# Rotary embedding on one core: GpSimd's two sine products per tile become one, and VectorE's program is padded to a 128-slot boundary

## The chip, the cores and the metric

The kernel runs on one core of a Trainium2 chip. The core has five engines with instruction streams of their own: TensorE (PE in the profile, its weight loads PEld), VectorE (DVE), ScalarE (ACT), GpSimd (POOL) and SyncE (SP). Sixteen DMA engines move data between the device memory (HBM) and the core's on-chip memory SBUF. PSUM is a second, smaller on-chip memory, which TensorE writes.

The metric is the device time of one execution in microseconds. Three runs of the kernel before gave 163.29, 163.35 and 163.39.

## The reference

The input `x` is float32 with 8 batches, 2048 positions, 8 heads and 64 elements per head. `cos` and `sin` have 32 elements per position. Each head's vector is split into halves and rotated:

```python
x1 = x[..., : x.shape[-1] // 2]
x2 = x[..., x.shape[-1] // 2 :]
out1 = x1 * cos - x2 * sin
out2 = x1 * sin + x2 * cos
return np.concatenate([out1, out2], axis=-1)
```

The input has 33.55 MB and the output as much.

## The kernel before, in words

The 2048 positions lie on the 128 partitions, 16 to a partition (`R` = 16). A batch is one SBUF buffer `xt` of 128 x 8192 elements, and there are five such buffers (`NBUF`). SyncE's queue loads batches 0 to 4 at the start, batch 0 in three pieces with the cosine table behind the first (lines 66 to 69); ScalarE's queue loads the sine table (line 76). Batch `b + 5` is loaded into the buffer of batch `b` once that batch has been stored (line 193). Stores go out on ScalarE's queue, and on SyncE's for the last batch (line 73). The first batch is stored in pieces of 1, 1 and 2 MB, the last in 2, 1 and 1 MB, the others as 4 MB.

A batch is worked off in tiles of 128 x 2048 elements (`UNIT`, four positions per partition). Batch 0 begins and batch 7 ends with two tiles of 128 x 1024 (lines 170 to 175). For each tile `rotate` makes two products and adds them. `t1` is `x` times the cosine, made by VectorE (line 129). `t2` is `x` with its halves exchanged, times the sine, with a minus sign in the first half of each head. In the usual kind of tile, A, GpSimd makes `t2` in two instructions (lines 120 to 127): the second half of each head is `x1` times `sin_sb`, the first half `x2` times `nsin`, which is the negated sine table. VectorE then adds `t1` and `t2` into `xt` (line 136). `t1` of such a tile lies in PSUM.

The first tile of each of batches 1 to 5 is of another kind. In kind B (batches 2, 4 and 5) TensorE makes the sum, as products with the identity `eye` that accumulate in PSUM, and ScalarE copies it back (lines 143 to 145). In kind C (batches 1 and 3) VectorE also makes the sine product (line 148) from a copy of the sine table in PSUM, and TensorE adds or subtracts with `eye` and `neye`. In B and C `t1`, and in C also `t2`, lie in the two SBUF buffers of the pool `t1s`.

GpSimd's `t2` tiles have three buffers (`t2_pool`), so GpSimd can run at most that far ahead of VectorE. The order of work is the order of the program on each engine (`keep`).

Before the loop, GpSimd makes the identity, ScalarE the negated sine table `nsin` (line 90), the PSUM copy `sin_ps` (line 91) and `neye` (line 92), and VectorE the PSUM copy of the cosine table (line 93).

Of the kernel before, what the change touches and what calls it, by code (L numbers as in the profile page):

```python
# [9 lines left out]
@with_exitstack  # L10
def kernel(
    ctx: ExitStack,
    tc: tile.TileContext,
    x: bass.AP,
    cos: bass.AP,
    sin: bass.AP,
    out: bass.AP,
):
    nc = tc.nc
    keep = tc.keep_in_program_order  # L20
    f32 = mybir.dt.float32
    PSUM = bass.MemoryType.PSUM

    B, S, H, D = x.shape
    Dh = D // 2
    P = 128
    HD = H * D
    R = S // P
    ROW = R * HD
    UNIT = 4 * HD  # L30
    NBUF = 5
    C = 512
    last = B - 1

    xv = x.rearrange("b (q r) h d -> b q (r h d)", q=P)
    ov = out.rearrange("b (q r) h d -> b q (r h d)", q=P)
    cos_src = cos.rearrange("(q r) d -> q r d", q=P)
    sin_src = sin.rearrange("(q r) d -> q r d", q=P)

    const_pool = ctx.enter_context(tc.tile_pool(name="const", bufs=1))  # L40
    tab_pool = ctx.enter_context(tc.tile_pool(name="tab", bufs=1, space=PSUM))
    t1_pool = ctx.enter_context(tc.tile_pool(name="t1p", bufs=1, space=PSUM))
    o_pool = ctx.enter_context(tc.tile_pool(name="op", bufs=1, space=PSUM))
    t1s_pool = ctx.enter_context(tc.tile_pool(name="t1s", bufs=2))
    xpool = ctx.enter_context(tc.tile_pool(name="xpool", bufs=NBUF))
    t2_pool = ctx.enter_context(tc.tile_pool(name="t2p", bufs=3))

    cos_sb = const_pool.tile([P, R, Dh], f32, tag="cb")
    sin_sb = const_pool.tile([P, R, Dh], f32, tag="sb")
    nsin = const_pool.tile([P, R, Dh], f32, tag="ns")  # L50
    eye = const_pool.tile([P, P], f32, tag="eye")
    neye = const_pool.tile([P, P], f32, tag="neye")
    cos_ps = tab_pool.tile([P, R, Dh], f32, tag="cp")
    sin_ps = tab_pool.tile([P, R, Dh], f32, tag="sp")

    xts = {}

    def spans(sizes):
        lo = 0
        for n in sizes:  # L60
            yield lo, n
            lo += n

    def load(b):
        xt = xpool.tile([P, ROW], f32, tag="xt", name=f"xt{b}")
        for lo, n in spans([UNIT, UNIT, 2 * UNIT] if b == 0 else [ROW]):
            keep(nc.sync.dma_start(out=xt[:, lo : lo + n], in_=xv[b, :, lo : lo + n]))
            if b == 0 and lo == 0:
                keep(nc.sync.dma_start(out=cos_sb, in_=cos_src))
        xts[b] = xt  # L70

    def store(b, lo, n):
        queue = nc.sync if b == last else nc.scalar
        keep(queue.dma_start(out=ov[b, :, lo : lo + n], in_=xts[b][:, lo : lo + n]))

    keep(nc.scalar.dma_start(out=sin_sb, in_=sin_src))
    for b in range(NBUF):
        load(b)

    keep(nc.gpsimd.memset(eye, 0.0))  # L80
    nc.gpsimd.affine_select(
        out=eye,
        in_=eye,
        compare_op=mybir.AluOpType.not_equal,
        fill=1.0,
        base=0,
        pattern=[[-1, P]],
        channel_multiplier=1,
    )
    keep(nc.scalar.mul(nsin, sin_sb, -1.0))  # L90
    keep(nc.scalar.copy(sin_ps, sin_sb))  # L91
    keep(nc.scalar.mul(neye, eye, -1.0))
    keep(nc.vector.tensor_copy(cos_ps, cos_sb))  # L93

    def rep(a, n):
        return dataclasses.replace(a, ap=[a.ap[0][:], a.ap[1][:], [0, n], a.ap[-1][:]])

    kinds = {}
    for b, kind in ((1, "C"), (2, "B"), (3, "C"), (4, "B"), (5, "B")):
        kinds[(b, 0)] = kind  # L100

    def rotate(b, lo, n):
        kind = kinds.get((b, lo), "A")
        xt = xts[b][:, lo : lo + n]
        r0 = lo // HD
        nr = n // HD
        xk = xt.rearrange("p (r k d) -> p r k d", r=nr, d=Dh)
        xu = xt.rearrange("p (g u d) -> p g u d", u=2, d=Dh)
        if kind == "A":
            t1 = t1_pool.tile([P, n], f32, tag="t1")  # L110
        else:
            t1 = t1s_pool.tile([P, n], f32, tag="t1s")
        if kind == "C":
            t2 = t1s_pool.tile([P, n], f32, tag="t1s")
        else:
            t2 = t2_pool.tile([P, n], f32, tag="t2")
        t1u = t1.rearrange("p (g u d) -> p g u d", u=2, d=Dh)
        t2u = t2.rearrange("p (g u d) -> p g u d", u=2, d=Dh)
        if kind != "C":
            for u, tab in ((1, sin_sb), (0, nsin)):  # L120
                keep(
                    nc.gpsimd.tensor_mul(  # L122
                        out=t2u[:, :, u, :].rearrange("p (r h) d -> p r h d", h=H),
                        in0=xu[:, :, 1 - u, :].rearrange("p (r h) d -> p r h d", h=H),
                        in1=rep(tab[:, r0 : r0 + nr, :], H),
                    )
                )
        keep(
            nc.vector.tensor_mul(  # L129
                out=t1.rearrange("p (r k d) -> p r k d", r=nr, d=Dh),  # L130
                in0=xk,
                in1=rep(cos_ps[:, r0 : r0 + nr, :], 2 * H),
            )
        )
        if kind == "A":
            keep(nc.vector.tensor_add(out=xt, in0=t1, in1=t2))  # L136
        elif kind == "B":
            for j in range(n // (2 * C)):
                o = o_pool.tile([P, 2 * C], f32, tag="o")
                for k in range(2):  # L140
                    cs = slice((2 * j + k) * C, (2 * j + k + 1) * C)
                    oc = o[:, k * C : (k + 1) * C]
                    nc.tensor.matmul(oc, eye, t1[:, cs], start=True, stop=False)  # L143
                    nc.tensor.matmul(oc, eye, t2[:, cs], start=False, stop=True)  # L144
                keep(nc.scalar.copy(xt[:, 2 * j * C : 2 * (j + 1) * C], o))  # L145
        else:
            keep(
                nc.vector.tensor_mul(  # L148
                    out=t2.rearrange("p (r k d) -> p r k d", r=nr, d=Dh),
                    in0=xk,  # L150
                    in1=rep(sin_ps[:, r0 : r0 + nr, :], 2 * H),
                )
            )
            G = C // Dh
            for u in range(2):
                o = o_pool.tile([P, n // 2], f32, tag="o")
                for j in range(n // 2 // C):
                    oc = o[:, j * C : (j + 1) * C]
                    gs = slice(j * G, (j + 1) * G)
                    nc.tensor.matmul(oc, eye, t1u[:, gs, u, :], start=True, stop=False)  # L160
                    nc.tensor.matmul(  # L161
                        oc, eye if u else neye, t2u[:, gs, 1 - u, :], start=False, stop=True
                    )
                keep(
                    nc.scalar.copy(  # L165
                        xu[:, :, u, :], o.rearrange("p (g d) -> p g d", d=Dh)
                    )
                )

    def pieces(b):  # L170
        if b == 0:
            return [2 * HD, 2 * HD, UNIT, UNIT, UNIT]
        if b == last:
            return [UNIT, UNIT, UNIT, 2 * HD, 2 * HD]
        return [UNIT] * 4

    def shares(b):
        if b == 0:
            return [UNIT, UNIT, 2 * UNIT]
        if b == last:  # L180
            return [2 * UNIT, UNIT, UNIT]
        return [ROW]

    for b in range(B):
        done = 0
        outs = list(spans(shares(b)))
        for lo, n in spans(pieces(b)):
            rotate(b, lo, n)
            done = lo + n
            while outs and sum(outs[0]) <= done:  # L190
                store(b, *outs.pop(0))
        if b + NBUF <= last:
            load(b + NBUF)
# [30 lines left out]
```

## Time and profile before

| | |
|---|---|
| median of three runs | 163.35 us |
| the profiled execution's own time | 163.35 us |
| its span, first to last instruction | 161.5 us |
| VectorE busy | 140.1 us, 87% of the span, 66 instructions |
| GpSimd busy | 138.9 us, 86%, 70 instructions |
| TensorE busy (matmuls) | 49.2 us, 30% |
| ScalarE busy | 12.8 us, 8% |
| DMA | 67.65 MB, mean 419 GB/s over the span |
| share of the 16 DMA engines' span | 55.3% on SyncE's queue (q1), 42.8% on ScalarE's (q10) |
| instruction packets (q14) | 2, 0.02 MB |

The profile page cuts the span into 40 equal slices. A digit in such a row is the busy share of a slice in tenths, and 9 stands for 90% or more. The row of the DMA is the mean over the 16 DMA engines. In the list of groups each line has the source line, the engine, the operation, the tiles written and read, the count, the busy time and mean, and the idle time ahead of the group with what ended it. An answer on the DMA for a short window has the same kind of rows, for slices of that window, and counts the packets that start in it. Instruction packets are transfers that bring program code to an engine; they run on the same 16 DMA engines as the data.

### The profile page before, as it was taken

How to read it: one execution, taken by the hardware profiler on the slowest of the kernel's cores; microseconds unless marked ns; L12 is line 12 of the kernel's file. 1: busy time of each engine (PE TensorE's matmuls, PEld its weight loads, DVE VectorE, ACT ScalarE, POOL GpSimd, SP SyncE). 2: the span in 40 equal slices, each digit the busy share in tenths (PEclk: the TensorE clock that was granted, in tenths of full speed). 3: DMA queues.
4: the chain of work that ended last, by engine and by line, in shares of the span. 5: the costliest groups of instructions: out<-in, count | busy, mean ns of one | idle time of the engine just before them, and what ended most of it. 6: DMA issues, size and time to landing. Idle time of an engine off the chain costs nothing.

```text
span 161.5 us, 460 instructions
## 1 busy us (share of the span) xinstructions
PE 49.2 (30%) x80; PEld 18.5 (11%) x80; DVE 140.1 (87%) x66; ACT 12.8 (8%) x14; POOL 138.9 (86%) x70
## 2 busy tenths in 40 slices
PE   0000000597309770978039723973000000000000
PEld 0000000142004220323023302320000000000000
DVE  0297999999999999999999999999999999999600
ACT  3300000002200220021100220022000000000000
POOL 1399997999999999999994999999999999996000
PEclk9999999999975998589956995599655555555555
DMA  5999998998999999999999999999999999999994
GB/s 153 423 458 418 430 487 381 430 487 381 487 398 446 389 462 389 462 446 389 487 422 389 487 416 389 487 422 398 473 422 406 471 422 406 471 422 406 426 404 209
DMA packets 3458, 67.65 MB, mean 419 GB/s; under 512 B 384, under 2 KB 384, under 8 KB 640
## 3 DMA queue, kind: packets, MB, share of 16 engines
q1 hardware_dynamic: 2016, 38.01, 55.3%
q10 hardware_dynamic: 1440, 29.62, 42.8%
q14 instruction: 2, 0.02, 0.0%
HBM read 34.08 MB, written 33.55 MB: 419 GB/s over the span
## 4 chain that ended last, share of the span: by engine, by line
DVE 75%; POOL 9%; issue 6%; DMA 4%; DVEq 0%
DVE t L129 40%; DVE xt L136 33%; POOL t L122 9%; DMA sin_sb<-in_sin_dram 4%; DVE t L148 3%; DVEq L136 0%
## 5 line engine op out<-in xcount | busy, mean ns | idle before, releaser
L122 POOL TENSOR_TENSOR t<-xt,sin_sb 128x1024 f32<-128x1024 f32 (+1 forms) x32 | 71.2, 2226 | 8.5 <-DMA sin_sb<-in_sin_dram 5.3
L129 DVE TENSOR_TENSOR t<-xt,cos_ps 128x2048 f32<-128x2048 f32 (+1 forms) x34 | 73.4, 2166 | 0.8
L122 POOL TENSOR_TENSOR t<-xt,nsin 128x1024 f32<-128x1024 f32 (+1 forms) x32 | 71.3, 2228 | 0.0
L136 DVE TENSOR_TENSOR xt<-t,t 128x2048 f32<-128x2048 f32 (+1 forms) x29 | 62.2, 2145 | 4.2 <-POOL t L122 1.2
L143 PE MATMUL o<-t,eye 128*128 128x512 f32 x24 | 16.9, 797 | 23.1 <-DVE t L129 19.7
L160 PE MATMUL o<-t,eye 128*128 128x512 f32 x16 | 12.0, 842 | 37.9 <-DVE t L129 35.7
L144 PE MATMUL o<-t,eye 128*128 128x512 f32 x24 | 14.9, 709 | 0.0
L145 ACT COPY xt<-o 128x1024 f32<-128x1024 f32 x6 | 6.1, 1012 | 45.7 <-PE o L144 45.7
L143 PEld LDWEIGHTS o<-t,eye 128*128 128x128 f32 x24 | 5.5, 256 | 32.5 <-issue 26.6
L160 PEld LDWEIGHTS o<-t,eye 128*128 128x128 f32 x16 | 3.7, 256 | 43.4 <-issue 39.5
L165 ACT COPY xt<-o 128x1024 f32<-128x1024 f32 x4 | 4.0, 1012 | 47.8 <-PE o L161 47.8
L93 DVE COPY cos_ps<-cos_sb 128x512 f32<-128x512 f32 x1 | 0.7, 695 | 7.1 <-DMA cos_sb<-in_cos_dram 7.1
L144 PEld LDWEIGHTS o<-t,eye 128*128 128x128 f32 x24 | 5.6, 235 | 8.1 <-issue 8.1
L161 PE MATMUL o<-t,neye 128*128 128x512 f32 x8 | 6.2, 872 | 0.2
L148 DVE TENSOR_TENSOR t<-xt,sin_ps 128x2048 f32<-128x2048 f32 x2 | 4.6, 2280 | 0.0
L161 PE MATMUL o<-t,eye 128*128 128x512 f32 x8 | 4.1, 592 | 0.0
L161 PEld LDWEIGHTS o<-t,neye 128*128 128x128 f32 x8 | 2.1, 296 | 5.2 <-issue 3.6
L161 PEld LDWEIGHTS o<-t,eye 128*128 128x128 f32 x8 | 1.5, 190 | 1.9 <-issue 1.9
L90 ACT ACT_TABLE_LOAD x1 | 1.3, 1283 | 1.2 <-PEq L208 1.2
L90 ACT ACTIVATE nsin<-sin_sb 128x512 f32<-128x512 f32 x1 | 0.6, 630 | 4.1 <-DMA sin_sb<-in_sin_dram 4.1
L91 ACT COPY sin_ps<-sin_sb 128x512 f32<-128x512 f32 x1 | 0.6, 578 | 0.0
L80 POOL MEMSET eye<- 128x128 f32 x1 | 0.2, 204 | 0.3 <-POOLq L208 0.3
(6 smaller groups left out, 1.0 us busy)
## 6 DMA issues: line engine op xcount, KB each, us to landing
xt<-in_x_dram SPq DMA_DIRECT2D x7, 4096.0 KB, 34.5
out_dram<-xt ACTq DMA_DIRECT2D x6, 4096.0 KB, 30.5
xt<-in_x_dram SPq DMA_DIRECT2D x2, 1024.0 KB, 6.8
xt<-in_x_dram SPq DMA_DIRECT2D x1, 2048.0 KB, 12.3
out_dram<-xt ACTq DMA_DIRECT2D x2, 1024.0 KB, 19.3
out_dram<-xt ACTq DMA_DIRECT2D x1, 2048.0 KB, 28.0
out_dram<-xt SPq DMA_DIRECT2D x1, 2048.0 KB, 13.5
out_dram<-xt SPq DMA_DIRECT2D x2, 1024.0 KB, 9.9
```

Source lines behind the costliest of these rows:

```text
L90: keep(nc.scalar.mul(nsin, sin_sb, -1.0))
L93: keep(nc.vector.tensor_copy(cos_ps, cos_sb))
L122: nc.gpsimd.tensor_mul(out=t2u[:, :, u, :].rearrange("p (r h) d -> p r h d", h=H), in0=xu[:, :, 1 - u, :].rearrange("p (r h) d -> p r h d" ...
L129: nc.vector.tensor_mul(out=t1.rearrange("p (r k d) -> p r k d", r=nr, d=Dh), in0=xk, in1=rep(cos_ps[:, r0 : r0 + nr, :], 2 * H),)
L136: keep(nc.vector.tensor_add(out=xt, in0=t1, in1=t2))
L143: nc.tensor.matmul(oc, eye, t1[:, cs], start=True, stop=False)
L144: nc.tensor.matmul(oc, eye, t2[:, cs], start=False, stop=True)
L145: keep(nc.scalar.copy(xt[:, 2 * j * C : 2 * (j + 1) * C], o))
L148: nc.vector.tensor_mul(out=t2.rearrange("p (r k d) -> p r k d", r=nr, d=Dh), in0=xk, in1=rep(sin_ps[:, r0 : r0 + nr, :], 2 * H),)
L160: nc.tensor.matmul(oc, eye, t1u[:, gs, u, :], start=True, stop=False)
L161: nc.tensor.matmul(oc, eye if u else neye, t2u[:, gs, 1 - u, :], start=False, stop=True)
L165: nc.scalar.copy(xu[:, :, u, :], o.rearrange("p (g d) -> p g d", d=Dh))
```

## The change

It has four parts. First, the sine table is kept as `sgn`, in which each position has the negated sine and then the sine, interleaved; ScalarE makes it in two instructions, and `nsin` is gone. Second, GpSimd makes `t2` of a tile in one instruction. It reads `x` with a backward step of 32 elements between the halves of a head, which exchanges them, and reads `sgn` for both halves at once. The very first tile keeps two products, from `sin_sb` and from the first half of `sgn`. Third, `cos_sb` and `sin_sb` are put into the two buffers of the pool `t1s` instead of buffers of their own. Fourth, `addr_align(128)` stands in front of VectorE's program in the kernel: when the program is loaded, empty instruction slots are put there so that the next instruction, the cosine copy, lies on a boundary of 128 slots of 64 bytes each. VectorE runs through these empty slots.

```diff
-    cos_sb = const_pool.tile([P, R, Dh], f32, tag="cb")
-    sin_sb = const_pool.tile([P, R, Dh], f32, tag="sb")
-    nsin = const_pool.tile([P, R, Dh], f32, tag="ns")
+    cos_sb = t1s_pool.tile([P, R, Dh], f32, tag="t1s", name="cos_sb")
+    sin_sb = t1s_pool.tile([P, R, Dh], f32, tag="t1s", name="sin_sb")
+
+    sgn = const_pool.tile([P, R, 2, Dh], f32, tag="sg")
...
+    keep(nc.vector.addr_align(128))
     keep(nc.gpsimd.memset(eye, 0.0))
...
-    keep(nc.scalar.mul(nsin, sin_sb, -1.0))
+    keep(nc.scalar.mul(sgn[:, :, 0, :], sin_sb, -1.0))
+    keep(nc.scalar.copy(sgn[:, :, 1, :], sin_sb))
     keep(nc.scalar.copy(sin_ps, sin_sb))
...
     def rep(a, n):
-        return dataclasses.replace(a, ap=[a.ap[0][:], a.ap[1][:], [0, n], a.ap[-1][:]])
+        return dataclasses.replace(a, ap=[a.ap[0][:], a.ap[1][:], [0, n]] + [d[:] for d in a.ap[2:]])
...
-        if kind != "C":
-            for u, tab in ((1, sin_sb), (0, nsin)):
+        if (b, lo) == (0, 0):
+            for u, tab in ((1, sin_sb), (0, sgn[:, :, 0, :])):
                 keep(
                     nc.gpsimd.tensor_mul(
...
+        elif kind != "C":
+            x5 = xt.rearrange("p (r h u d) -> p r h u d", r=nr, h=H, u=2)
+            dims = [d[:] for d in x5.ap[:3]] + [[-Dh, 2], x5.ap[4][:]]
+            keep(
+                nc.gpsimd.tensor_mul(
+                    out=t2.rearrange("p (r h u d) -> p r h u d", r=nr, h=H, u=2),
+                    in0=dataclasses.replace(x5, offset=x5.offset + Dh, ap=dims),
+                    in1=rep(sgn[:, r0 : r0 + nr], H),
+                )
+            )
```

## The prediction

> **What bounds the kernel now.** I read the page's slices first, because two engines look like the bound there, and then asked the DMA answers whether the last stage belongs to them.
>
> ```profile
> DVE  0297999999999999999999999999999999999600
> POOL 1399997999999999999994999999999999996000
> DMA  5999998998999999999999999999999999999994
> q14 instruction: 2, 0.02, 0.0%
> L136 DVE TENSOR_TENSOR xt<-t,t 128x2048 f32<-128x2048 f32 (+1 forms) x29 | 62.2, 2145 | 4.2 <-POOL t L122 1.2
> ```
>
> VectorE and GpSimd are full for 37 of 40 slices, but both stop at slice 37 while the DMA row goes on: the engines end, the stores do not. The busy time by stretches has the DMA share and GB/s in its last two columns:
>
> ```profile
> 10.00:40.00 30.00, 8.52 (x13) 3.14 (x14) 28.46 (x15) 1.01 (x1) 29.15 (x15) 1.00 1.01 435
> 146.00:158.00 12.00, 0.00 (x0) 0.00 (x0) 5.92 (x5) 0.00 (x0) 2.02 (x2) 0.50 1.01 430
> 158.00:161.50 3.50, 0.00 (x0) 0.00 (x0) 0.00 (x0) 0.00 (x0) 0.00 (x0) 0.50 0.41 173
> ```
>
> Early with loads alone, and late with stores alone, the 16 DMA engines are fully busy at about 432 GB/s (in the packet records a 32 KB packet takes 1.213 us on one engine: 27.0 GB/s, times 16). So transfers bound the kernel from about 2 us to 159 us, although the chain of waits gives VectorE 75%. VectorE ends at 152.2. After 140 us the DMA still moves 8.26 MB, 19.1 us at 432 GB/s, and the last 1 MB of it (2.4 us) need not start before 156.7. The store of it is issued at 152.2, and at the start of the run issue to first packet took 1.0 us: VectorE could be 3.4 us later and nothing would starve.
>
> What ends last inside the DMA? The final 2.5 us, in slices of 62.5 ns (a packet is counted where it starts, and a 3 is one 8 KB packet):
>
> ```profile
> DMA  3999666300060000300000000000000000000000
> ```
>
> Fourteen engines start their last packet by 159.44 and end by 159.74. Two engines are late: the packet records end them at 160.03 and at 160.37. The last one holds up the final store, and the span ends 1.1 us after it. Where did they fall behind? The only other traffic is the two instruction packets, one in each of these stretches (93 to 95 us, then 115 to 117 us):
>
> ```profile
> q14 instruction: 1, 0.01, 1.0%
> ...
> q14 instruction: 1, 0.01, 1.0%
> ```
>
> Following the packets engine by engine (each starts as its predecessor ends), the engine that ends at 160.37 carried the 8 KB instruction packet at 94.09 (0.31 us), and its next 32 KB packet took 1.745 us where others took 1.213: 0.84 us lost. The one that ends at 160.03 carried the packet at 115.84, and its next took 1.434: 0.53 us lost. An engine that is always busy never wins that back. Without the packets they would have ended at 159.53 and 159.50.
>
> Whose are they? 8192 bytes are 128 slots of 64. GpSimd's program has about 96 instructions, VectorE's about 116, the most of the engines except TensorE. At 92.6 (1.5 us ahead of the first packet) VectorE was at about its 71st instruction and GpSimd at its 62nd; at 113.8 (2.0 us ahead of the second) at the 83rd and the 73rd. Whichever owns which, each passes one 128-slot boundary if some 45 to 66 slots precede the kernel. TensorE had only matmuls already queued at 92 and had finished by 110; I count it out with less certainty.
>
> **The change part by part.** The sum is made against the profiled execution: 163.35 us, which is also the median of the runs; span 161.5 and 1.85 outside it.
>
> *GpSimd's product.* Products follow each other every 2.28 us at 1024 elements and every 1.215 at 512, so 1024 more cost 2.13, and one product of 2048 should take 2.28 + 2.13 = 4.41 us where a pair takes 4.56. No row has one with a backward step; bounds: 4.41, and no gain over the slowest pair, 2 x 2.32 = 4.64. I take 4.41: each half already jumps every 32 elements, which the pair shows to cost nothing per element beyond 2.08 ns. 28 full tiles and 3 half ones save 31 x 0.15 = 4.6 us of GpSimd. What it releases: VectorE's wait for GpSimd of 0.85 us at 16.1 shrinks by 0.3, the one of 0.33 at 102.0 goes. VectorE then ends 0.6 us earlier, and the stores are issued earlier into a queue that is full anyway: worth 0. At 4.64 also 0, hidden by the 3.4 us above and the 2.1 us for which GpSimd waits on its three buffers at 85.8.
>
> *ScalarE.* One more copy of 512 elements, 0.58 us (row L91). It ends at 7.7 us; GpSimd's first use of the table's second half is at 9.1, so 1.4 us cover it. The sine copy for PSUM and the negated identity end at 8.3 and 8.6; first uses are at 30 and 32 us, and ScalarE's next store is at 13.0. Zero.
>
> *The tables in the two t1s buffers.* VectorE's first products into them stand at 27.8 and 30.0 us; the last reader of a table there ends at 9.1. Zero, and SP's and ScalarE's transfers keep their order.
>
> *The padding.* At most 127 empty slots on VectorE between its release at 0.69 us and its first copy at 7.06. No row shows an empty slot; the nearest are semaphore instructions on VectorE, 21 ns busy and 69 ns from one to the next. With 45 to 57 slots ahead and 4 in the kernel there are 67 to 79 of them, 1.4 to 5.5 us: done by 6.2, behind the wait for the cosine table. Were that cover gone (127 x 69 ns = 8.8 us, to 9.5), VectorE would start 2.4 us late, less than its 3.4. Zero.
>
> *The instruction packets.* GpSimd's program shrinks by 31 instructions to 65 in all; its boundary at about the 62nd or 73rd then lies behind the final barrier, which it reaches as its 59th, or past its end. One packet goes. VectorE's boundary moves to the end of the padding; from there 114 instructions fit below the next one. So its packet moves from after 90 us to 2.1 to 6.2 us plus 1.5 to 2.0, about 4 to 8 us, when the DMA is full already. It costs its engine at least the bare 0.31; the two late ones cost 0.53 and 0.84, each behind a 32 KB packet. At 4 to 8 us packets are of 8 KB and less, and the one disturbed there (at 5.03 us) took 0.395 instead of 0.309. That row is nearest, so I take 0.31 + 0.09 rounded up, 0.42; ends 0.31 and 0.84, and 0 if it comes before the DMA is full. A gain beyond 0.63 is excluded, for the other engines end at 159.74.
>
> Sum: that engine ends at 159.50 + 0.42 = 159.92 instead of 160.37: -0.45 us, 162.90.
>
> [...]
>
> **The rivals.**
> - *No packet delays anything* (VectorE's comes before the DMA is full, or not at all): the others' 159.74 sets the end, -0.63, 162.72. For it: the ramp up to about 3 us. Against: the padding must then take under 1 us.
> - *No gain*: a packet of someone else's (TensorE), or the early one costs 0.84 like the worst: the end stays at 160.34 to 160.37, 163.3 to 163.35. [...] For it: the 0.84 was seen; ownership is inferred from counts.
> - *Slower, by GpSimd's new product.* Its place is GpSimd's row; it decides once a product costs over 4.86: the 2.96 us by which GpSimd's end (148.02) precedes its last reader (150.98), 3.4 and 2.1 make 8.5 over 28 tiles, 0.30 each on 4.56. At 5.2 us the end moves by 28 x 0.34 = 9.5: 172.9. Against: 2.08 ns per element whatever the jumps.
> - *Slower, by padding that draws one packet more* onto the same DMA engine: 0.42 + 0.84 = 160.76, +0.39, 163.74.
>
> **How the numbers follow.** Forecast 0.42, no delay 0.15, no gain 0.28, slow product 0.06, extra packet 0.09. About 0.2% (0.33 us) is what a measurement can tell from no change. The forecast's own range, 0.31 to 0.53, gives -0.56 to -0.34: faster, with the second case 0.57; same 0.28; slower 0.15. The range 162.65 to 163.5 holds the first three cases (0.85) with some 0.1 us of scatter, as in the three runs.
>
> **What would show it.** The instruction queue with no packet after 10 us; the last slices with at most one late engine; products every 4.4 us and no wait of VectorE for GpSimd at 102; VectorE ending near 151.6. I am wrong if an instruction packet remains after 90 us, if products exceed 4.86, or if the DMA rate itself changes.

## The result, and the profile after

The changed kernel took 163.78 us (median of 9 executions, 163.58 to 163.95). The kernel before, run beside it, took 163.40 (9 executions, 163.29 to 163.66). The ratio is 1.0021, with a 95% interval from 1.0013 to 1.0030. The change made the kernel slower by 0.2%; 0.3% faster had been forecast. Some executions, of the kernel before too, are longer than the rest for a reason that stays open (of 29 of before in the last comparison, 7 took 164.1 to 164.5 us and the others 163.2 to 163.6); the ratios below count them, the medians hardly do. The profiled execution of the changed kernel took 163.95 us and its span is 162.0, 0.5 us more than before.

First the page, with the lines that answer to those shown of before:

```profile
DVE  0298999999999999999999999999899998999600
POOL 1399994999999999989996999997999969998000
DMA  5999799899999999999989999999989999989893
q14 instruction: 1, 0.01, 0.0%
L135 POOL TENSOR_TENSOR t<-xt,sgn 128x2048 f32<-128x2048 f32 (+1 forms) x31 | 132.7, 4312 | 7.4 <-DMA xt<-in_x_dram 5.5
L149 DVE TENSOR_TENSOR xt<-t,t 128x2048 f32<-128x2048 f32 (+1 forms) x29 | 62.2, 2144 | 4.7 <-POOL t L135 2.0
```

One instruction packet is left of two. VectorE does the same additions in the same time (62.2 us). GpSimd is busy 135.9 us where it was 138.9. The stages, busy time by stretches with DMA share and GB/s last:

```profile
10.00:40.00 30.00, 8.88 (x14) 3.38 (x15) 28.68 (x15) 1.01 (x1) 27.58 (x7) 1.00 1.00 430
146.00:158.00 12.00, 0.00 (x0) 0.00 (x0) 6.20 (x5) 0.00 (x0) 3.07 (x2) 0.50 1.00 428
158.00:161.50 3.50, 0.00 (x0) 0.00 (x0) 0.00 (x0) 0.00 (x0) 0.00 (x0) 0.50 0.41 171
```

The DMA engines are full in the same stretches and at nearly the same rate (430 and 428 GB/s; before 435 and 430). So the bound is the same, and the question is again which DMA engine ends last. VectorE's empty slots (count, duration, first and last start), the instruction queue between 7.0 and 8.5 us, and the DMA between 159.0 and 161.5 us in slices of 62.5 ns:

```profile
L81 DVEq NOP  x61: 18/18/18, 0.8 to 3.6; - x61
```

```profile
q14 instruction: 1, 0.01, 1.3%
```

```profile
DMA  9939363000300003000030003000000000000000
```

The padding is 61 slots, 47 ns apart, and ends at 3.6 us. The packet records put the one packet at 7.49 us. In the last row the 3s that stand alone, four to five slices apart, are 8 KB packets of one engine: the last starts at 160.56 and ends at 160.87. Before, the last 3 stood at 160.0 and its packet ended at 160.37. The other fifteen engines end by 159.74, as fourteen did before. Following the packets engine by engine, the one that carried the instruction packet lost 0.31 us by the packet and 0.61 by its next packet, of 8 KB, which took 0.92 instead of 0.309. Slow 32 KB packets follow in the same chain of packets at 24.9, 42.1, 72.0, 91.5 and 111.0 us (0.13 to 0.26 each). Where two packets end at the same instant the records don't say which engine goes on with which, so these can't all be booked to one engine. Nor would they simply add: they make 0.93 us, and ordinary engines meet slow packets too (the 32 KB packets of all 16 engines together took 6.2 us more than 1.213 each before, and 8.8 after). The end itself can be booked: against its natural end of some 159.50 this engine is 1.37 us late, 0.92 by the packet and its next, 0.45 by what came later.

### The profile page after: what moved, and what is told of

The parts are those of the page before. It is cut to its first block, busy times and chain, and to the rows that moved or that the text cites. A ratio compares the mean times of both kernels' runs of the same rounds, so it can differ in the third digit from the quotient of the medians.

```text
span 162.0 us, 492 instructions
## 1 busy us (share of the span) xinstructions
PE 48.3 (30%) x80; PEld 18.1 (11%) x80; DVE 140.1 (86%) x66; ACT 13.3 (8%) x15; POOL 135.9 (84%) x39
## 4 chain that ended last, share of the span: by engine, by line
DMA 46%; DVE 37%; POOL 9%; issue 2%; DVEq 0%; SPq 0%; POOLq 0%; ACTq 0%
DMA xt<-in_x_dram 22%; DMA out_dram<-xt 20%; DVE t L142 18%; DVE xt L149 17%; POOL t L135 7%; DMA sin_sb<-in_sin_dram 4%; POOL t L125 2%; DVE t L161 1%; DVEq L149 0%; SPq L68 0%; POOLq L135 0%; ACTq L75 0%
## 5 line engine op out<-in xcount | busy, mean ns | idle before, releaser
L135 POOL TENSOR_TENSOR t<-xt,sgn 128x2048 f32<-128x2048 f32 (+1 forms) x31 | 132.7, 4312 | 7.4 <-DMA xt<-in_x_dram 5.5
L149 DVE TENSOR_TENSOR xt<-t,t 128x2048 f32<-128x2048 f32 (+1 forms) x29 | 62.2, 2144 | 4.7 <-POOL t L135 2.0
L156 PE MATMUL o<-t,eye 128*128 128x512 f32 x24 | 16.4, 771 | 23.7 <-DVE t L142 20.2
L173 PE MATMUL o<-t,eye 128*128 128x512 f32 x16 | 11.7, 822 | 37.7 <-DVE t L142 35.5
L157 PE MATMUL o<-t,eye 128*128 128x512 f32 x24 | 14.9, 709 | 0.0
L125 POOL TENSOR_TENSOR t<-xt,sin_sb 128x512 f32<-128x512 f32 x1 | 1.3, 1283 | 5.2 <-DMA sin_sb<-in_sin_dram 5.2
L174 PE MATMUL o<-t,eye 128*128 128x512 f32 x8 | 4.1, 592 | 0.0
L125 POOL TENSOR_TENSOR t<-xt,sgn 128x512 f32<-128x512 f32 x1 | 1.3, 1269 | 0.0
L92 ACT ACTIVATE sgn<-sin_sb 128x512 f32<-128x512 f32 x1 | 0.6, 630 | 4.0 <-DMA sin_sb<-in_sin_dram 4.0
L93 ACT COPY sgn<-sin_sb 128x512 f32<-128x512 f32 x1 | 0.6, 601 | 0.0
```

What stands on the lines that cost most here:

```text
L92: keep(nc.scalar.mul(sgn[:, :, 0, :], sin_sb, -1.0))
L125: nc.gpsimd.tensor_mul(out=t2u[:, :, u, :].rearrange("p (r h) d -> p r h d", h=H), in0=xu[:, :, 1 - u, :].rearrange("p (r h) d -> p r h d" ...
L135: nc.gpsimd.tensor_mul(out=t2.rearrange("p (r h u d) -> p r h u d", r=nr, h=H, u=2), in0=dataclasses.replace(x5, offset=x5.offset + Dh, ap ...
L174: nc.tensor.matmul(oc, eye if u else neye, t2u[:, gs, 1 - u, :], start=False, stop=True)
```

## The experiments

Two theories stood at first. By one, the early packet costs more than forecast and is the whole loss. By the other, GpSimd's new product, or a changed order of transfers, has its own part in it. All runs were timed against the kernel before on the chip that ran them. Every profiled execution, of before, of after and of the eleven runs below other than j, k and l, has one thing in common: its time is the end of its last packet plus 2.97 to 3.10 us (3.22 in f_short_vector). So the end of the last packet can be compared straight with the times.

| run | instruction packets at (us) | last packet ends | time of that execution | median (range) of all |
|---|---|---|---|---|
| before | 94.09, 115.84 | 160.37 | 163.35 | 163.41 (163.26 to 164.73) |
| after | 7.49 | 160.87 | 163.95 | 163.78 (163.58 to 163.95) |
| a_merge_only | 94.08 | 160.36 | 163.46 | 163.51 (163.35 to 164.90) |
| b_pad_only | 7.28, 113.40 | 160.15 | 163.12 | 163.63 (163.12 to 164.75) |
| c_branch | 3.77 | 161.32 | 164.40 | 164.25 (163.90 to 164.57) |
| d_late_boundary | 44.49 | 160.83 | 163.90 | 163.89 (163.50 to 164.80) |
| h_mid_boundary | 64.97 | 160.82 | 163.90 | 163.81 (163.40 to 164.62) |
| g_two_early | 6.76, 7.81 | 160.45 | 163.42 | 163.92 (163.42 to 164.52) |
| i_after_again | 7.54 | 160.43 | 163.52 | 163.74 (163.52 to 163.96) |
| f_short_vector | none | 160.95 | 164.17 | 164.31 (164.03 to 164.86) |
| m_no_packet | none | 160.46 | 163.54 | 163.23 (163.00 to 163.54) |
| n_early_packet | 7.24 | 161.12 | 164.20 | 163.81 (163.28 to 164.22) |
| o_middle_packet | 76.11 | 160.54 | 163.61 | 163.62 (163.41 to 163.96) |

The row of before has its first profiled execution, and the times that stand beside a to i.

### One part of the change alone: a_merge_only and b_pad_only

a_merge_only is the changed kernel without the padding:

```diff
-    keep(nc.vector.addr_align(128))
```

b_pad_only is the kernel before with the padding:

```diff
+    keep(nc.vector.addr_align(128))
     keep(nc.gpsimd.memset(eye, 0.0))
```

> The changed kernel without the padding. Straggler theory (the one DMA engine that carries an instruction packet ends last and sets the time): GpSimd's packet is gone, VectorE's stays near 94 us with about 0.84 us lost, so the last engine still ends near 160.37 and the time is that of before, 163.3 to 163.5. Rival (the new product or the tables in the shared buffers cost the time): 163.8, as after. If instead VectorE's packet was the one at 115.84, the time is 163.0.

> The kernel before with the padding alone. Straggler theory: VectorE's packet comes at about 7.5 us, GpSimd's stays at 94 or 116; the engine with the early one ends near 160.9, time 163.7 to 163.9. Rival (the product or the tables cost it): 163.4.

a_merge_only took 163.51 us, ratio 1.0016 (0.9996 to 1.0036). Its instruction queue between 93 and 95 us, and its DMA from 159.0 to 161.5:

```profile
q14 instruction: 1, 0.01, 1.0%
```

```profile
DMA  9999099600330000300000000000000000000000
```

The packet at 94.08, which cost 0.31 + 0.53 before, is there and costs the same; GpSimd's at 115.84 is gone. The last packet ends at 160.36 as before (160.37). So the packet at 94 is VectorE's, the one at 116 was GpSimd's (in b_pad_only, where VectorE alone is padded, it is the one at 94 that goes), and the merged product by itself is worth nothing measurable: the packet that it takes away sat on an engine that was not the last.

b_pad_only took 163.63, ratio 1.0024 (1.0005 to 1.0044). Its early packet at 7.28 lost 0.31 + 0.59 on its engine, GpSimd's at 113.40 lost 0.31 + 0.21. Of the 163.7 to 163.9 expected it fell just short. Its profiled execution was its fastest (163.12), with a DMA row that ends early:

```profile
DMA  9696996333330300000000000000000000000000
```

In this execution the engine with the early packet can be followed to its end with few doubtful steps (14 of 164). It lost 0.90 us at the packet and 0.13 and 0.23 in two later ones, at 24.3 and 50.3 us, and still ended at 160.15, only 0.65 after 159.50. So an engine's losses do not simply add to a fixed end.

The median is within 0.15 us of the changed kernel's, with the old products. Its interval lies above 1 and that of a_merge_only does not, so the loss goes with the padding. With differences of 0.1 to 0.3 us between medians that scatter as much, this is a leaning. The runs m, n and o below make firm that such a packet costs time, though not that an early one costs more than a late one.

### The place of the packet: c_branch, d_late_boundary, h_mid_boundary

The padding is made shorter, so that VectorE's program crosses the boundary later (33 and 18 empty slots), or is jumped over by a branch, so that it is crossed at once:

```diff
-    keep(nc.vector.addr_align(128))
+    keep(nc.vector.addr_align(128, max_nops=0))     # c_branch
+    keep(nc.vector.addr_align(128, offset=100))     # d_late_boundary
+    keep(nc.vector.addr_align(128, offset=85))      # h_mid_boundary
```

> The changed kernel, but VectorE branches over the 61 empty slots instead of running through them, so that it crosses the boundary at about 0.8 us instead of 3.6. Straggler theory: the packet comes 1.0 to 3.9 us later, at 1.8 to 4.7; if it comes before the DMA engines are full (about 2.2 us) nothing lags and the time is 162.7 to 162.9; at 3 to 4.7 it still lags by 0.3 to 0.9 and the time is 163.0 to 163.5. Rival (the product or the tables cost it): 163.8.

> The changed kernel with VectorE's program put 100 slots behind a boundary: 33 empty slots instead of 61, and the next boundary is crossed inside the batches, at about 37 us. Straggler theory with later losses (an engine that is out of step meets further slow packets): one packet near 40 to 44 us, 0.5 to 0.9 lost at once and up to 0.4 later, time 163.3 to 163.6, between before and after. Rival (only the loss at the packet counts, 0.84 to 0.92 wherever it is): 163.35 to 163.45. Rival (product or tables): 163.8.

> The changed kernel with VectorE's program put 85 slots behind a boundary: 18 empty slots, the next boundary is crossed at about 60 us and the packet should come near 65 to 70. Theory of later losses (0.84 us at the packet, then 0.1 to 0.3 at each of some batch boundaries that the late engine still has to pass): 163.5 to 163.7, between the packet at 94 us (163.5) and that at 44 us (163.9). Rival (only the loss at the packet counts): 163.4 to 163.5.

The branch stands where the empty slots were:

```profile
L81 DVEq COMPARE_BRANCH  x1: 47/47/47, 0.8 to 0.8; - x1
```

The last DMA rows, from 159.0 us as above, of c_branch, d_late_boundary and h_mid_boundary:

```profile
DMA  6999936906036000030000300003000030000000
```

```profile
DMA  6309933066000330000300003000000000000000
```

```profile
DMA  0999903333000030000300003000000000000000
```

Each has one engine far behind, whose 8 KB packets stand alone at the end. The packet and the next one cost 0.31 + 0.53 or 0.54 in all three, as at 94 us. The engine then met further slow packets: 0.19 and 0.22 in d_late_boundary, 0.29 and 0.23 in h_mid_boundary, and 0.98 in c_branch, where the packet came earliest (taken from the end of the engine; the single packets of c_branch can't all be told apart). All three took longer than the theory had expected: 163.89 for 163.3 to 163.6, 163.81 for 163.5 to 163.7, and 164.25 for at most 163.5. The 163.8 of the rival, that the product or the tables cost the time, would suit d and h; a_merge_only, which has the same product and tables and whose last packet ends at 160.36, speaks against it. The medians go mostly the same way: 163.51 (packet at 94), 163.81 (65), 163.89 (44), 164.25 (3.8); the changed kernel's repeat below, with 163.74 for a packet at 7.5, does not fit the order. The ratios are 1.0014 (0.9992 to 1.0036) for h_mid_boundary, 1.0030 (1.0014 to 1.0046) for d_late_boundary and 1.0039 (1.0021 to 1.0058) for c_branch, whose fastest execution (163.90) is 0.4 us above the fastest of the other two. That an early packet is dear because its engine is out of step for longer is argued from these rows, not shown.

### Two early packets, and the change once more: g_two_early and i_after_again

g_two_early pads GpSimd's program too; i_after_again is the changed kernel unaltered.

```diff
     keep(nc.vector.addr_align(128))
+    keep(nc.gpsimd.addr_align(128))
```

> The changed kernel with GpSimd's program padded to a boundary of 128 slots too, so that a second instruction packet comes in the first 10 us, on another DMA engine. Straggler theory (the latest single engine sets the end, losses on different engines do not add up): two late engines, time that of the changed kernel or up to 0.3 more, 163.8 to 164.1. Rival (each early packet costs the whole DMA 0.4 us): 164.2 to 164.3.

> The changed kernel once more, on the same chip as the other three: 163.7 to 164.0, packet near 7.5 us. It is there to be compared with them.

i_after_again took 163.74, ratio 1.0013 (0.9996 to 1.0031), beside 163.51 for the merge alone. The difference of 0.23 is inside the scatter of 12 executions each (-0.39 to 0.38 by resampling them). g_two_early took 163.92. Its two packets lost 0.31 + 0.29 and 0.31 + 0.60, on two engines, which are the two late ones at 160.20 and 160.45:

```profile
DMA  9609993096000330003000000000000000000000
```

The losses of the two engines do not add: the later one sets the end.

### No packet, with additions left out: f_short_vector

VectorE's program would have to be short enough to cross no boundary. In f_short_vector VectorE's additions in tiles of kind A are left out, the product with the cosine goes straight into `xt`, and there is no padding:

```diff
-                out=t1.rearrange("p (r k d) -> p r k d", r=nr, d=Dh),
+                out=xk if skip else t1.rearrange("p (r k d) -> p r k d", r=nr, d=Dh),
...
-            keep(nc.vector.tensor_add(out=xt, in0=t1, in1=t2))
```

> The changed kernel without the padding and with VectorE's additions of the kind-A tiles left out (VectorE writes x times cosine straight into xt, GpSimd's sine product is made and not used, so the output is not the rotation). VectorE's program in the kernel is 53 instructions instead of 109 and stays below the 128-slot boundary; every transfer of data is as before. Straggler theory: no instruction packet in the run, no late DMA engine, end of the last packet near 159.75 instead of 160.37, time 162.6 to 162.9. Rival (the packets are harmless and something else sets the last 0.6 us): 163.3 to 163.5.

It took 164.31, ratio 1.0049 (1.0032 to 1.0066): slower, with no instruction packet at all. Its DMA between 74 and 78 us, and from 159.0 to 161.5:

```profile
74.00:78.00 4.00, 2.11 (x3) 0.97 (x4) 1.74 (x1) 0.00 (x0) 4.00 (x2) 0.77 0.98 393
```

```profile
DMA  9996999939999393330633006330000000000000
```

From 74 to 78 us the DMA moved 393 GB/s, where from 10 to 40 us it moved 431. Nearly all engines are late here, not one: they end between 159.67 and 160.95. The 32 KB packets of all engines together took 20.3 us more than 1.213 each, most of it around 40, 75, 95 and 115 us; before it was 6.2. VectorE waited for GpSimd 63.9 us, which moved its stores in time; that this made the packets slow is likely and not shown. So the expectation failed, and the run does not test the packet: it changed the order of the transfers as well. It did bring a new rival: stalls of all engines could take the place of the packet whenever the timing shifts.

### No packet, with VectorE's time kept: j, k, l and then m, n, o

To keep VectorE's time with half the instructions, one instruction of twice the elements takes the place of product and sum in tiles of kind A; what these six runs store is not the rotation. Three runs have the same work and differ in the packet alone: none, early (61 empty slots), middle (31).

```diff
-                out=t1.rearrange("p (r k d) -> p r k d", r=nr, d=Dh),
...
-            keep(nc.vector.tensor_add(out=xt, in0=t1, in1=t2))
+            keep(nc.vector.tensor_add(out=halves, in0=twice(t2), in1=twice(t2)))    # j, k, l
+            keep(nc.vector.tensor_mul(out=halves, in0=twice, in1=table))            # m, n, o
...
+    keep(nc.vector.addr_align(128))                 # k, n
+    keep(nc.vector.addr_align(128, offset=98))      # l, o
```

> Left out, so that VectorE's program is too short to cross a boundary and its time stays: in the tiles that VectorE adds, product and sum are replaced by one instruction of twice the elements (GpSimd's product plus itself, written over the tile as 2 x 1024 two-byte values per 1024 four-byte ones, so all of the tile is stored as before). No padding. VectorE then has 53 instructions in place of 114, and no 8 KB instruction packet is expected. If the instruction packet is what held up the last DMA engine, all 16 engines end at 159.4 to 159.8 as the fifteen others do in the changed kernel (159.36 to 159.74), and the time is 162.6 to 162.9, 0.6 to 0.8 us under the kernel before. If the end is set by stalls that all engines meet when stores and loads shift, as in f_short_vector, it is 163.4 to 164.3 with no packet at all. If the new instruction does not take about 4.3 us (2 x 2.14), VectorE's pace differs, and only the comparison with the two runs beside it counts.

> As j_no_packet (the same work left out), with VectorE's program padded to a boundary of 128 slots as in the changed kernel, 61 empty slots ahead of its first instruction. One instruction packet is expected at 7 to 8 us. By the theory of the packet: its DMA engine loses 0.9 us there and up to 0.7 more in the following batches, ends at 160.4 to 160.9, and the time is 0.7 to 1.2 us over j_no_packet. By the rival, that the whole order of transfers sets the end, it differs from j_no_packet by under 0.3 us, in either direction.

> As j_no_packet (the same work left out), with 31 empty slots, so that VectorE crosses the boundary in the middle of its work. One instruction packet is expected at 80 to 105 us. By the theory of the packet: its engine loses 0.84 us there and little more afterwards, as in the kernel before, and the time is 0.5 to 0.8 us over j_no_packet and 0 to 0.5 us under k_early_packet. By the rival it differs from both by under 0.3 us.

j_no_packet took 261.89 us, k_early_packet 261.85, l_middle_packet 261.84 (ranges 261.69 to 262.11). The page of j_no_packet, the DMA row and the groups of GpSimd and VectorE:

```profile
DMA  7999999997999781979393003900077000391643
```

```profile
L134 POOL TENSOR_TENSOR t<-xt,sgn 128x2048 f32<-128x2048 f32 x28 | 196.0, 7028 | 30.5 <-DVE xt L154 30.5
L154 DVE TENSOR_TENSOR xt<-t 128x4096 bf16<-128x4096 f32 x25 | 184.6, 7427 | 28.8 <-POOL t L134 28.8
```

With both of VectorE's inputs in SBUF, GpSimd's product took 7.03 us instead of 4.52, and VectorE's instruction 7.43. The engines became the bound and the DMA had gaps. So these runs missed their purpose, but they show one thing: the packet at 7.80 in k and the one at 120.53 in l cost nothing to within 0.3 us where the DMA is not the bound.

> As j_no_packet, but the one long VectorE instruction per tile reads GpSimd's product and the cosine table in PSUM, so only one of its inputs is in SBUF, as in the product and the sum that it stands for (left out: the sum; what is stored is product times table as 2 x 1024 two-byte values). VectorE has 53 instructions and no padding: no instruction packet is expected. If it takes 4.3 to 4.5 us and GpSimd's product stays at 4.4, the DMA is the bound again. Then by the theory of the packet all 16 engines end within 0.4 us of each other and the time is 162.5 to 163.0; by the rival, that stalls met by all engines set the end, it is 163.4 to 164.3 without any packet.

> As m_no_packet with VectorE padded to the boundary (61 empty slots): one packet at 7 to 8 us. By the theory of the packet: one DMA engine ends 0.8 to 1.5 us after the others and the time is 0.7 to 1.2 us over m_no_packet. By the rival: within 0.3 us of m_no_packet. If the DMA has slack, as in j_no_packet, there is no difference by either.

> As m_no_packet with 31 empty slots: one packet at 80 to 105 us. By the theory of the packet: 0.5 to 0.8 us over m_no_packet and 0 to 0.5 us under n_early_packet. By the rival: within 0.3 us of both.

With one input in PSUM, both engines are back at their pace, 4.3 us in the mean over full and half tiles for GpSimd and 4.1 for VectorE (m_no_packet's page):

```profile
L134 POOL TENSOR_TENSOR t<-xt,sgn 128x2048 f32<-128x2048 f32 (+1 forms) x31 | 132.7, 4312 | 5.1 <-DMA xt<-in_x_dram 3.4
L156 DVE TENSOR_TENSOR xt<-t,cos_ps 128x4096 bf16<-128x4096 f32 (+1 forms) x29 | 119.0, 4124 | 9.3 <-POOL t L134 7.3
```

m_no_packet took 163.23 (163.00 to 163.54), n_early_packet 163.81 (163.28 to 164.22), o_middle_packet 163.62 (163.41 to 163.96), 12 executions each on one chip. The early packet costs 0.57 us (95% by resampling: 0.15 to 0.92), the middle one 0.39 (0.17 to 0.59). Early against middle, 0.19, is not resolved (-0.19 to 0.50). Against the kernel before, m_no_packet is the only kernel whose interval lies below 1: ratio 0.9971 (0.9952 to 0.9989). By the medians it is 0.23 us faster (163.23 against 163.46). The last DMA rows of m, n and o from 159.0 us:

```profile
DMA  6969663333030300303000000000000000000000
```

```profile
DMA  6699633366030330300300003000300000000000
```

```profile
DMA  9993999003300033000300000000000000000000
```

So the packet does move the time, with the same work and a full DMA, though by less than the 0.7 to 1.2 and 0.5 to 0.8 that were expected, and m_no_packet itself is not at 163.0 or under. The row of m says why. That profiled execution was the slowest of its twelve, and two engines are late in it, at 160.32 and 160.46, with no instruction packet anywhere. One of them has a 32 KB packet at 113.9 that took 0.44 us too long while no other engine's did. It is not alone: n and o have one instruction packet each and two late engines, so that in n an engine without one ended at 160.32 or later, in o at 160.26 or later. Data packets are late by themselves now and then in these runs, and the end is that of the latest of 16 engines. A packet's 0.84 or 0.92 counts only by what it stands out over that.

m, n and o leave work out, so no run here is a complete kernel that beats both. a_merge_only is as fast as the kernel before within the measurement.

## Why the prediction was wrong, step by step

*The bound* was right: a full DMA up to 159 us, and time = end of the last packet + 3 us in every profiled execution with a full DMA.

*GpSimd's product* was right in that it is hidden, and too large in size. The first product of the first and of the eleventh pair in a row before, and ten products in a row after:

```profile
26.09 2.33 POOL L122 TENSOR_TENSOR t<-xt,sin_sb 128x1024 f32<-128x1024 f32 x1 [0.85 <-DMA xt<-in_x_dram]
71.92 2.43 POOL L122 TENSOR_TENSOR t<-xt,sin_sb 128x1024 f32<-128x1024 f32 x1
```

```profile
27.12 44.92 POOL L135 TENSOR_TENSOR t<-xt,sgn 128x2048 f32<-128x2048 f32 x10 [2.42 <-DMA xt<-in_x_dram]
```

The products take 4.49 us each, not 4.41; the ten pairs before, from 26.09 to 71.92, took 4.58. So 0.09 us is saved per tile where 0.15 was forecast. What it releases was wrong: the wait at 102 is gone, but VectorE's waits for GpSimd came to 2.0 us in four (1.2 in two before), since GpSimd now waits 5.5 us for loads. VectorE ended at 152.5, not 151.6. It cost nothing, for the 3.4 us of cover held.

*ScalarE's copy, the tables and the padding* were zero as forecast. The padding was 61 slots (67 to 79 forecast), 47 ns each, done by 3.6 us; the cosine copy started at 6.9.

*The instruction packets.* Number and place were right: one was GpSimd's and went, one was VectorE's and moved to 4 to 8 us (7.49). The step that failed is the next one, "I take 0.31 + 0.09 rounded up, 0.42; ends 0.31 and 0.84". The early packet measured 0.31 + 0.61 = 0.92 in the profile after, and 0.89 to 0.92 in b_pad_only, g_two_early, i_after_again and n_early_packet. The row taken as nearest, the packet at 5.03 that took 0.395 instead of 0.309, had not been shown to follow an instruction packet, and it was preferred to the two rows that did, only because it was of the same size and nearer in time. Of those two, the packet that moved was VectorE's, the one at 94 that had cost 0.84. With 0.92 in the sum the engine ends at 159.50 + 0.92 = 160.42, and the time is 163.40: no gain. The profiled execution's other 0.45 us (160.87) is outside the sum altogether: "an engine that is always busy never wins that back" was taken as a constant loss, while the lag grew in c, d and h by 0.4 to 1.0 after the packet, and in b_pad_only was smaller at the end than at the packet (0.65 and 0.90). What makes it grow or shrink stays open. A further assumption was never asked, that without a packet the end would be 159.74: m_no_packet's median of 163.23 lies at 160.2 by the same 3 us.

*The rivals.* "No gain" named the mechanism, the early packet that "costs 0.84 like the worst", with 0.28; the slower case was given to a second packet on the same engine, which did not occur. What was missing is that the packet that moved earlier could cost its engine more than the one it replaced (0.92 us against 0.84). That a packet might cost nothing held only where the DMA is not full (k_early_packet and l_middle_packet, within 0.3 us of j_no_packet); with a full DMA it cost 0.39 us in o_middle_packet and 0.57 in n_early_packet, against m_no_packet.

*What stays open:* why the packet behind an instruction packet is slow by 0.2 to 0.6 us, and how far the extra loss of an early packet is its place and how far chance. That the changed kernel gained nothing is explained by the price of the packet; that it lost 0.2% rests on the profile after and on leanings.

## What to carry to other kernels

In these runs, j, k and l aside, the 16 DMA engines were full up to about 159 us, and the time was the end of the latest engine plus 2.97 to 3.22 us. An 8 KB instruction packet and the packet behind it, some 0.84 to 0.92 us on a single engine, showed up in the total with 0.39 us (o_middle_packet) and 0.57 (n_early_packet), while 3.0 us less of GpSimd's busy time (138.9 to 135.9 in a_merge_only) did not show: GpSimd had cover. Moving VectorE's packet did not make it cheaper here: 0.84 us at 94 us became 0.92 at 7.5. Taking away GpSimd's, on an engine that was not the last, gained nothing. Price a cost of this kind by the rows that show the same event, not by a row that looks alike nearby, and ask what the next latest engine would be before booking the whole difference.

## What the runs showed that was not expected

- An instruction packet was issued well after its boundary was crossed: 3.9 us after the end of the padding (3.6 to 7.49), 3.0 us after the branch of c_branch (0.8 to 3.77). 1.5 to 2.0 had been assumed.
- The packet behind it lost 0.53 us in five places from 3.8 to 94 us, 0.59 to 0.61 at 7 to 8 us (0.29 for the first of two in g_two_early), and 0.21 to 0.22 at 113 to 116 us. Place alone does not sort these: in l_middle_packet it lost 0.53 at 120.5 us. The owner does. All of 0.53 and more are VectorE's packets; those at 113 and 116 are GpSimd's, and so, by the end of its padding (3.1 us against 3.6), is probably the first of g_two_early. Why is not shown.
- With both of VectorE's inputs in SBUF (j_no_packet) GpSimd's product took 7.03 us, and VectorE's instruction of 4096 elements 7.43. With one of them in PSUM VectorE's took 4.42 (the 25 of that size in m_no_packet), and GpSimd's product 4.52 (the 28 of that size in the changed kernel; over both sizes its mean there and in m_no_packet is the same, 4.31). VectorE's instruction also adds in j and multiplies in m; why both engines are slow in j alone is not shown.
